# Emptying the product banks of gates and output projection through ScalarE

## The chip, the cores and the metric

The kernel runs on one core of a Trainium2 chip. The metric is the device time of one execution in microseconds (us). The engines are named as in the profile: PE is TensorE (matmuls and transposes), PEld its weight loads, DVE is VectorE, ACT is ScalarE, POOL is GpSimd, SP is SyncE, which issues DMAs here. PE writes only to PSUM, which has eight banks of 128 x 512 float32 in this kernel's use; a bank can be written anew when everything that reads its old content is done.

## The reference

One layer of a decoder trunk with 1024 tokens and 1024 features, all in float32:

```python
h = rms_norm(x, norm_in_gain) * (1.0 + scale) + shift        # scale, shift, gate from silu(c) @ w_ada
q, k, v, z_attn, xbc, dt_raw, z_ssm = split(h @ w_in)
o = stick_breaking_attention(q, k, v)                        # 16 heads of 64
y_attn = rms_norm(o, sb_norm_gain) * silu(z_attn)
xs, b, c = split(silu(causal_depthwise_conv(xbc)))
y = ssd_scan(xs, softplus(dt_raw), a, b, c, d_skip)          # 16 heads, chunks of 128
y_ssm = rms_norm(y * silu(z_ssm), ssm_norm_gain)
x = x + gate * (concat([y_attn, y_ssm]) @ w_out)
return rms_norm(x, norm_f_gain)
```

The attention weight of query t on key s is sigmoid(z_ts) times the product of (1 - sigmoid(z_tj)) over s < j < t.

## The kernel before

Every product with a weight matrix is made of three float32r matmuls (high x high, high x low, low x high parts), 128 x 128 weights against 512 columns, accumulated over eight k tiles. `inproj_f` makes one 128-row block of the input projection: two banks (`b` = 0, 1), eight k-steps of three matmuls each, and after each bank its `evac`. `inproj_v` makes the value columns, `outproj` the output projection.

Up to about 305 us the kernel computes the normalised input, the convolution inputs and the state-space scan. From then on (`pinned[0] = True`) every instruction stands in the order in which the program emits it on its engine. That order comes from a loop over the eight pairs of heads, `ROUND`: `scores(p, i)` makes the logits of query block i in the four `pz` banks, ScalarE turns them into two sigmoids (queue `late["A"]`), VectorE scans the products along the keys and multiplies (`scan`, `weights`, queue `late["V"]`). `turned(p, i)` transposes the weights on PE and ScalarE copies them back, `values(p, i)` multiplies them with v. Between these, `fill` and `side_step` run the side jobs of `SIDES`, one k-step at a time: `z` (attention gate), `g` (SSM gate, in round 0 only), `q` (q and k of the next pair), `v`, in round 6 `t` (`turn`, the last gate with the exchange of h for w_out in SBUF) and in round 7 `o` (`out_ssm`, the SSM half of the output projection). The attention half follows after the loop. `after(delay, fn)` emits something when the planner's clock `tick` has gone on by `delay`; `late` items are emitted at a planned rate per engine.

PSUM banks are in four pools: `pj` has two banks, for all projections; `pz` four, for the scores; `pt` and `pv` one each, for transposes and for the attention's values. A `turned` of more than four 128-column blocks ("wide") needs a second bank besides `pt` and takes it from `pj`. When it may start is a rule on `left`, the planned time that the projection bank in work still needs:

```python
            while wide and side_left() and left[0] >= 0.0 and not 1.3 < left[0] < (2.2 if slow[0] else 3.6):
                side_step()
```

`slow` is set by the jobs whose bank VectorE empties (`by_v=True` of `zgate` and `gate_ssm`, and `outproj`). Such a bank has two readers: ScalarE's sigmoid or tanh, and VectorE's product with it (line 959 and line 848); of `out_ssm` it has one, VectorE's product with a row statistic and the gate (line 1227). Banks of q and k (`qk`) are read by two ScalarE instructions when pinned: the high part and a full copy into the buffer `th`, and VectorE subtracts from the copy.

`turn` holds two `pj` banks (`pss`) at once, since it goes over the k tiles once to free h: as each k is done for both banks, `split_w` writes rows of w_out in its place. The first bank of `out_ssm` is taken from `pz`, and the loop holds `scores(7, 7)` back until that bank's evacuation is emitted (`hooks["first"]`).

Of the kernel before, what the change touches and what calls it, by code (L numbers as in the profile page):

```python
# [8 lines left out]
F32 = mybir.dt.float32  # L9
# [5 lines left out]
P = 128  # L15
# [11 lines left out]
def hybrid_layer_kernel(  # L27
# [66 lines left out]
    def bank(pool, tag):  # L94
        return mk(pool, tag, [P, HALF])

    eps_t = const("eps_t", [P, 2])
# [83 lines left out]

    left, slow = [0.0], [False]

    h_hi, h_lo = [None] * KT, [None] * KT

# [105 lines left out]
            K(T.matmul(ps, w[:, ws], h[:, b * HALF:(b + 1) * HALF],  # L295
                       start=(k == 0 and n == 0), stop=(k == KT - 1 and n == 2)))

    def inproj_f(col, evac, between=None, by_v=False):


        wts = take(2) if pinned[0] else split_f(load_f(col))
        for b in range(2):
            ps = bank(pj, "pj")
            for k in range(KT):
                mm_f(ps, wts, k, b)
                if pinned[0]:
                    ahead()
                    if b and k % 4 == 3:
                        used()
                left[0], slow[0] = 0.7 * (KT - 1 - k), by_v  # L310
                yield 0.7
            evac(b, ps)
            if between:
                yield between(b)

    def inproj_v(vc, with_dt, v_tiles, dt_raw, extra=None):

        n = 272 if with_dt else 256
        wts = {}
        if not with_dt:  # L320
            for q, (whi, wlo) in enumerate(take(4)):
                for k in range(2):
                    wts[2 * q + k] = (whi, wlo, slice(k * n, (k + 1) * n))
        else:
            for k0 in range(0, KT, 2):
                raw = wraw()
                rv = raw[:, :2 * n].rearrange("p (k f) -> p k f", f=n)
                rs = slice(k0 * P, (k0 + 2) * P)
                SP.dma_start(rv[:, :, :256], w_in[0][rs, C_V + vc * 256:C_V + (vc + 1) * 256]
                             .rearrange("(k p) f -> p k f", p=P))  # L330
                SP.dma_start(rv[:, :, 256:272], w_in[0][rs, C_DT:C_DT + 16]
                             .rearrange("(k p) f -> p k f", p=P))
                whi, wlo = split(raw, 2 * n)
                for k in range(2):
                    wts[k0 + k] = (whi, wlo, slice(k * n, (k + 1) * n))
        for i in range(TB):
            ps = bank(pj, "pj")
            ts_ = slice(i * P, (i + 1) * P)
            for k in range(KT):
                whi, wlo, ws = wts[k]  # L340
                K(T.matmul(ps[:, :n], h_hi[k][:, ts_], whi[:, ws], start=(k == 0), stop=False))  # L341
                K(T.matmul(ps[:, :n], h_hi[k][:, ts_], wlo[:, ws], start=False, stop=False))  # L342
                if i == 0 and extra:
                    extra(ps[:, n:n + TB], k)
                K(T.matmul(ps[:, :n], h_lo[k][:, ts_], whi[:, ws], start=False, stop=(k == KT - 1)))  # L345
                if not with_dt:
                    ahead()
                    if i == TB - 1 and k % 2:
                        used()
                if k == 3:  # L350
                    left[0], slow[0] = 1.4, False
                    yield 1.4
            if i == 0 and extra:
                extra(ps[:, n:n + TB], KT)
            for j in range(2):
                A.copy(v_tiles[j][:, i * P:(i + 1) * P], ps[:, j * P:(j + 1) * P])
            if with_dt:
                A.copy(dt_raw[:, i, :], ps[:, 256:272])
            left[0] = 0.0
            yield 1.4  # L360
# [479 lines left out]
    def gate_ssm(j):  # L840
        box = []

        def evac(b, ps):
            if b == 0:
                box.append(mk(sp, "th", [P, S], bufs=1))
            th, sl = box[0], slice(b * HALF, (b + 1) * HALF)
            A.activation(th[:, sl], ps, AF.Tanh, scale=0.5)
            V.scalar_tensor_tensor(th[:, sl], th[:, sl], 1.0, ps, op0=ALU.add, op1=ALU.mult)
            V.tensor_tensor(xs[j][:, sl], xs[j][:, sl], th[:, sl], op=ALU.mult)

        yield from inproj_f(C_ZS + j * P, evac, by_v=True)
        if pinned[0]:
            after(4.0, lambda: gated(j))
        else:
            gated(j)
# [73 lines left out]
    def qk(p, box):  # L929

        parts = []

        def evac(b, ps):
            if b == 0:
                parts.extend((big(F32R), big(F32R)))
            hi, lo = parts[-2:]
            sl = slice(b * HALF, (b + 1) * HALF)
            A.copy(hi[:, sl], ps)
            if pinned[0]:

                full = mk(sp, "th", [P, S], bufs=1)[:, sl]
                A.copy(full, ps)
                V.tensor_tensor(lo[:, sl], full, hi[:, sl].bitcast(F32), op=ALU.subtract)
            else:
                V.tensor_tensor(lo[:, sl], ps, hi[:, sl].bitcast(F32), op=ALU.subtract)

        for base in (C_Q, C_K):
            yield from inproj_f(base + p * P, evac, gate_row if p == 7 and base == C_Q else None)
        box[p] = parts
# [3 lines left out]
    def zgate_evac(p):  # L953
        def evac(b, ps):
            if b == 0:
                zgs[p] = mk(sp, "bc", [P, S], bufs=4)
            zg = zgs[p][:, b * HALF:(b + 1) * HALF]
            A.activation(zg, ps, AF.Sigmoid)
            V.scalar_tensor_tensor(zg, zg, cols[:, 92 + p:93 + p], ps, op0=ALU.mult, op1=ALU.mult)

        return evac

    def zgate(p):
        yield from inproj_f(C_Z + p * P, zgate_evac(p), by_v=True)

# [77 lines left out]
    def turned(p, i):  # L1045
# [2 lines left out]

        while banks:
            wide = sum(b[2] - b[1] for b in banks[:2]) > 4  # L1050
            while wide and side_left() and left[0] >= 0.0 and not 1.3 < left[0] < (2.2 if slow[0] else 3.6):
                side_step()
            n = 1 if wide and left[0] < 0.0 else 2
            go, banks = banks[:n], banks[n:]
# [57 lines left out]
        A.copy(gate, pg)  # L1112
        return 1.1

    def outproj(w_h, w_l, evac, first=None):

        yt = take(2)
        for b in range(2):
            ps = first if first is not None and b == 0 else bank(pj, "pj")
            sl = slice(b * HALF, (b + 1) * HALF)  # L1120
            for k in range(KT):
                yh, yl = yt[k // 4]
                ks = slice(k % 4 * P, (k % 4 + 1) * P)
                for n, (y, w) in enumerate(((yh, w_h), (yh, w_l), (yl, w_h))):
                    K(T.matmul(ps, y[:, ks], w(k, b), start=(k == 0 and n == 0), stop=(k == KT - 1 and n == 2)))  # L1125
                ahead()
                if b and k % 4 == 3:
                    used()
                left[0], slow[0] = 0.7 * (KT - 1 - k), True
                if k == KT - 1:  # L1130
                    evac(sl, ps)
                yield 0.7
# [8 lines left out]
    def turn():  # L1141
# [46 lines left out]
                load_half(0, lambda q: hp.tile([P, 2, HALF], F32, tag=f"hl{q}", name=f"wor{q}"))  # L1188


        for k, b in [(k, b) for k in range(6) for b in range(2)] + [(6, 0), (7, 0), (6, 1), (7, 1)]:
            for n in range(2):
                K(T.matmul(pss[b], wts[k // 4][n][:, k % 4 * P:(k % 4 + 1) * P],
                           h_hi[k][:, b * HALF:(b + 1) * HALF], start=False, stop=(k == KT - 1 and n == 1)))
            ahead()
            if b:
                wo_h[k] = hp.tile([P, S], F32R, tag=f"hh{k}", name=f"woh{k}")
                split_w(k, 0, V)
                if k % 4 == 3:
                    used()  # L1200
            yield 0.47
            if k == KT - 1:
                zgate_evac(7)(b, pss[b])
# [9 lines left out]
    def out_ssm():  # L1213
# [6 lines left out]
        for i in range(TB):  # L1220
            t3 = []

            def evac(sl, ps):
                hooks["first"] = True
                if not t3:
                    t3.append(mk(sp, "v", [P, S], bufs=3))
                V.scalar_tensor_tensor(t3[0][:, sl], ps, rstds["s"][:, i:i + 1], row["sum"][:, sl],
                                       op0=ALU.mult, op1=ALU.mult)

            yield from outproj(lambda k, b: wo_h[k][:, b * HALF:(b + 1) * HALF],  # L1230
                               lambda k, b: wo_l[k // 2, b][:, k % 2], evac, None if i else bank(pz, "pz"))
            if not x_at:
                load_x2(i)
            t2 = x_at.pop(i)
# [133 lines left out]
    for p in range(9):  # L1368
        for what, i, before in ROUND:
# [4 lines left out]
            elif what == "t":  # L1374
                turned(p + before, i)
            elif what == "f":
                fill(2.0)
            else:
                while p not in box:
                    side_step()  # L1380
                while (p, i) == (7, 7) and "first" not in hooks:
                    side_step()
                scores(p, i)
                fill(4.0 if i != 3 else 2.0)
            if (p, what, i) == (6, "f", 0):
# [126 lines left out]
```

## Time and profile before

| | |
|---|---|
| time, median of 3 runs | 1063.65 us (1063.28 to 1064.63) |
| the profiled execution | 1063.0 us, span of its instructions 1061.3 us |
| granted TensorE clock | 0.999 |
| PE busy | 1039.0 us (98%) |
| DVE busy | 768.0 us (72%) |
| ACT busy | 528.6 us (50%) |
| DMA | 96.15 MB, mean 91 GB/s |
| rounds p = 1 to 7 begin at | 411, 493, 563, 633, 703, 773 and 850 us |

The profile is one execution, recorded on the chip. "Busy" of PE counts pipelined matmuls whose ends are modelled, so short waits hide in it; where it matters, the distance between the starts of two matmuls is taken instead. Nearly all instructions of ACT, DVE and SP carry line 62 (L62), a helper, so groups are told apart by the names of what they write and read: `bc<-bc,cols,pj` writes tile `bc` from `bc`, `cols` and bank `pj`. Of PE, L295 are the input projections, L341 to L345 the values' projection, L1003 the scores, L1066 the transposes of `turned`, L1084 the attention's values, L1182 and L1193 `turn`, L1125 the output projection.

### The profile page before, as it was taken

What the parts mean: (1) busy time and instruction counts of PE and PEld (TensorE: products, weight loads), DVE (VectorE), ACT (ScalarE), POOL (GpSimd) and SP (SyncE); (2) the same over time, 40 slices, a digit from 0 to 9 for tenths busy, and PEclk for the clock granted to TensorE, in tenths of its full rate; (3) what the DMA queues carried; (4) which work ended last, traced back from release to release, by engine and by line L of the source; (5) the groups of instructions that cost most, each with busy time, mean ns of one, the idle gap of its engine ahead of it and who ended that gap; (6) DMA issues with size and microseconds to landing.
All of it is one profiled execution on the core that took longest, in us unless ns stands there. A gap on an engine that the chain in (4) does not pass through costs nothing.

```text
span 1061.3 us, 16252 instructions
## 1 busy us (share of the span) xinstructions
PE 1039.0 (98%) x6317; PEld 844.2 (80%) x6317; DVE 768.0 (72%) x1339; ACT 528.6 (50%) x1162; POOL 2.6 (0%) x23
## 2 busy tenths in 40 slices
PE   7999999999999999999999999999999999999997
PEld 5789888777877787798787987878977777688886
DVE  5728779988848775656787758877668789665554
ACT  5755397676423553563554644646546646410111
POOL 0000000000000000000000000000000000000000
PEclk9999999999999999999999999999999999999999
DMA  9611332223202221101321103211111632665432
GB/s 350 229 41 31 92 112 79 74 95 129 71 20 70 80 70 31 60 21 41 91 59 61 31 21 90 76 35 41 39 52 30 199 97 74 204 210 174 155 110 79
DMA packets 91560, 96.15 MB, mean 91 GB/s; under 512 B 5998, under 2 KB 75994, under 8 KB 91484
## 3 DMA queue, kind: packets, MB, share of 16 engines
q1 hardware_dynamic: 88828, 86.45, 25.9%
q10 hardware_dynamic: 2656, 8.67, 2.4%
q8 instruction: 49, 0.80, 0.3%
q14 instruction: 27, 0.22, 0.1%
HBM read 78.26 MB, written 16.84 MB: 90 GB/s over the span
## 4 chain that ended last, share of the span: by engine, by line
PE 86%; DVE 8%; ACT 2%; issue 2%; DMA 1%; ACTq 0%; DVEq 0%; SPq 0%
PE pj L295 35%; PE pj L1125 13%; PE pv L1084 6%; PE pz L1003 5%; PE pz L553 3%; PE pt L1066 3%; PE pj L345 3%; PE pj L341 3%; PE pj L342 3%; DVE om L62 2%; PE pj L1066 2%; DVE bc L62 2%; PE pz L815 1%; PE pv L829 1%; PE pz L820 1%
## 5 line engine op out<-in xcount | busy, mean ns | idle before, releaser
L295 PE MATMUL pj<-hh,whi 128*128 128x512 f32 x544 | 222.2, 408 | 0.0
L295 PE MATMUL pj<-hh,wlo 128*128 128x512 f32 x544 | 214.1, 394 | 0.0
L295 PE MATMUL pj<-hl,whi 128*128 128x512 f32 x544 | 212.5, 391 | 0.0
L295 PEld LDWEIGHTS pj<-hh,whi 128*128 128x128 f32 x544 | 102.3, 188 | 24.5 <-issue 5.6
L295 PEld LDWEIGHTS pj<-hh,wlo 128*128 128x128 f32 x544 | 102.1, 188 | 22.7 <-issue 0.7
L295 PEld LDWEIGHTS pj<-hl,whi 128*128 128x128 f32 x544 | 102.5, 188 | 19.1 <-issue 1.0
L62 DVE TENSOR_TENSOR wlo<-raw,whi 128x512 fp32r<-128x512 f32 (+1 forms) x109 | 75.4, 692 | 23.1 <-ACT whi L62 16.7
L62 ACT COPY be<-pt 128x512 f32<-128x512 f32 (+2 forms) x98 | 47.1, 499 | 82.7 <-PE pt L1066 79.7
L62 ACT ACTIVATE be<-pz 128x255 f32<-128x255 f32 (+5 forms) x160 | 84.6, 531 | 0.0
L62 DVE TENSOR_TENSOR_SCAN om<-om 128x896 f32<-128x896 f32 (+6 forms) x56 | 71.9, 1285 | 2.0
L62 DVE TENSOR_TENSOR_SCAN bc<-bc 128x896 f32<-128x896 f32 (+6 forms) x56 | 71.9, 1285 | 2.0
L62 DVE TENSOR_TENSOR_SCAN om<-om,ident 128x128 f32<-128x128 f32 x64 | 26.9, 421 | 62.3 <-ACT om L62 62.2
L62 ACT ACTIVATE om<-pz 128x512 f32<-128x512 f32 (+1 forms) x96 | 48.0, 500 | 36.1 <-PE pz L1003 36.1
L341 PE MATMUL pj<-whi,hh 128*128 128x256 f32 (+1 forms) x224 | 65.1, 291 | 0.0
L1003 PE MATMUL pz<-big,big 64*128 64x512 f32 (+2 forms) x576 | 63.5, 354 | 1.1 <-ACT be L62 0.9
L345 PE MATMUL pj<-whi,hl 128*128 128x256 f32 (+1 forms) x224 | 64.4, 288 | 0.0
L342 PE MATMUL pj<-wlo,hh 128*128 128x256 f32 (+1 forms) x224 | 63.6, 284 | 0.0
L62 ACT ACTIVATE th<-v 128x1024 f32<-128x1024 f32 (+2 forms) x9 | 8.5, 943 | 103.7 <-DVE v L62 103.7
L1003 PEld LDWEIGHTS pz<-big,big 64*128 64x128 f32 x576 | 46.2, 184 | 17.3 <-issue 10.2
L62 DVE TENSOR_TENSOR be<-be,bc 128x1024 f32<-128x1024 f32 (+6 forms) x62 | 55.4, 894 | 1.3
L295 PE MATMUL pj<-hh,st 128*128 128x512 f32 x160 | 55.4, 399 | 0.0
L62 ACT ACTIVATE bc<-pz 128x512 f32<-128x512 f32 (+1 forms) x96 | 53.7, 559 | 0.0
(303 smaller groups left out, 2166.8 us busy)
## 6 DMA issues: line engine op xcount, KB each, us to landing
raw<-in_w_in_dram SPq DMA_DIRECT2D x98, 256.0 KB, 2.8
be<-acT_d ACTq DMA_DIRECT2D x16, 512.0 KB, 3.8
big<-in_x_dram SPq DMA_DIRECT2D x10, 512.0 KB, 6.9
aw<-in_w_ada_dram SPq DMA_DIRECT2D x16, 256.0 KB, 4.6
u_d<-big SPq DMA_DIRECT2D x8, 512.0 KB, 2.6
y_d<-bc SPq DMA_DIRECT2D x8, 512.0 KB, 3.0
raw<-in_w_ada_dram SPq DMA_DIRECT2D x16, 256.0 KB, 2.7
raw<-u_d SPq DMA_DIRECT2D x16, 256.0 KB, 2.9
```

Of the source, the lines that this page charges most:

```text
L62: return lambda *args, **kw: K(op(*args, **kw))
L295: K(T.matmul(ps, w[:, ws], h[:, b * HALF:(b + 1) * HALF], start=(k == 0 and n == 0), stop=(k == KT - 1 and n == 2)))
L341: K(T.matmul(ps[:, :n], h_hi[k][:, ts_], whi[:, ws], start=(k == 0), stop=False))
L342: K(T.matmul(ps[:, :n], h_hi[k][:, ts_], wlo[:, ws], start=False, stop=False))
L345: K(T.matmul(ps[:, :n], h_lo[k][:, ts_], whi[:, ws], start=False, stop=(k == KT - 1)))
L553: K(T.matmul(acc[f][:, c0:c1], w[:, f * P:(f + 1) * P], h[:, sl], start=(k == 0 and n == 0 and c0 == 0), stop=(k == KT - 1 and n == 2)))
L815: K(T.matmul(po, xd[:, 0, h, :], m[:, h, :], start=True, stop=(ch == 0)))
L820: K(T.matmul(po, st[:, h, :], abc[:, h, :], start=False, stop=True))
L1003: K(T.matmul(zs[b][e][:, z0:z0 + mw], a[r, i * P:(i + 1) * P], k_[r, c0:c0 + mw], start=(n == 0), stop=(n == 2)))
L1066: K(T.transpose(room[:, (used_ + j - j0) * P:(used_ + j - j0 + 1) * P], be[:, j * P:(j + 1) * P], ident))
L1084: K(T.matmul(pav[p][64 * e:64 * e + 64, (q0 + u) * P:(q0 + 2) * P], vs[p][:, j * P + 64 * e:j * P + 64 * e + 64], tl[e][:, u:2, x0 + j * P ...
L1125: K(T.matmul(ps, y[:, ks], w(k, b), start=(k == 0 and n == 0), stop=(k == KT - 1 and n == 2)))
```

## The change

A helper `emptied` copies a bank to a new two-fold SBUF buffer `hf` on ScalarE, with a per-row scale where one is given. The products of `zgate_evac`, of `gate_ssm` (where pinned) and of `out_ssm` read the copy instead of the bank; `qk` uses the helper for the copy that it had. The `slow` flag goes, and with it the narrower rule for a wide `turned`. The first bank of `out_ssm` comes from `pj`, and `scores(7, 7)` no longer waits for its evacuation. In `turn` the last three k tiles go over the first bank and then over the second, and `split_w` of the first half is emitted 1.2 us later on the planner's clock. The scratch space for dynamic DMA is halved.

```diff
+    def emptied(ps, scale=None):
+        full = mk(sp, "hf", [P, HALF], bufs=2)
+        if scale is None:
+            A.copy(full, ps)
+        else:
+            A.activation(full, ps, AF.Copy, scale=scale)
+        return full
...
-                left[0], slow[0] = 0.7 * (KT - 1 - k), by_v
+                left[0] = 0.7 * (KT - 1 - k)
...
             A.activation(th[:, sl], ps, AF.Tanh, scale=0.5)
-            V.scalar_tensor_tensor(th[:, sl], th[:, sl], 1.0, ps, op0=ALU.add, op1=ALU.mult)
+            full = emptied(ps) if pinned[0] else ps
+            V.scalar_tensor_tensor(th[:, sl], th[:, sl], 1.0, full, op0=ALU.add, op1=ALU.mult)
...
             A.copy(hi[:, sl], ps)
             if pinned[0]:
-                full = mk(sp, "th", [P, S], bufs=1)[:, sl]
-                A.copy(full, ps)
-                V.tensor_tensor(lo[:, sl], full, hi[:, sl].bitcast(F32), op=ALU.subtract)
+                V.tensor_tensor(lo[:, sl], emptied(ps), hi[:, sl].bitcast(F32), op=ALU.subtract)
...
             A.activation(zg, ps, AF.Sigmoid)
-            V.scalar_tensor_tensor(zg, zg, cols[:, 92 + p:93 + p], ps, op0=ALU.mult, op1=ALU.mult)
+            V.scalar_tensor_tensor(zg, zg, cols[:, 92 + p:93 + p], emptied(ps), op0=ALU.mult, op1=ALU.mult)
...
-            while wide and side_left() and left[0] >= 0.0 and not 1.3 < left[0] < (2.2 if slow[0] else 3.6):
+            while wide and side_left() and left[0] >= 0.0 and not 1.3 < left[0] < 3.6:
...
-            ps = first if first is not None and b == 0 else bank(pj, "pj")
+            ps = bank(pj, "pj")
...
-        for k, b in [(k, b) for k in range(6) for b in range(2)] + [(6, 0), (7, 0), (6, 1), (7, 1)]:
+        for k, b in ([(k, b) for k in range(5) for b in range(2)] + [(k, 0) for k in range(5, KT)]
+                     + [(k, 1) for k in range(5, KT)]):
...
-                split_w(k, 0, V)
+                after(1.2, lambda k=k: split_w(k, 0, V))
...
-                V.scalar_tensor_tensor(t3[0][:, sl], ps, rstds["s"][:, i:i + 1], row["sum"][:, sl],
-                                       op0=ALU.mult, op1=ALU.mult)
+                full = emptied(ps, rstds["s"][:, i:i + 1])
+                V.tensor_tensor(t3[0][:, sl], full, row["sum"][:, sl], op=ALU.mult)
...
-                while (p, i) == (7, 7) and "first" not in hooks:
-                    side_step()
...
-    nc = _bacc.Bacc("TRN2", target_bir_lowering=False, num_devices=1, dynamic_dma_scratch_size=8192)
+    nc = _bacc.Bacc("TRN2", target_bir_lowering=False, num_devices=1, dynamic_dma_scratch_size=4096)
```

More of the change, by code (lines that the diff above doesn't have):

```diff
@@ L182, in weave @@
                 live.remove(it)
-    left, slow = [0.0], [False]
+    left = [0.0]
     h_hi, h_lo = [None] * KT, [None] * KT
@@ L296, in mm_f, with inproj_f @@
                        start=(k == 0 and n == 0), stop=(k == KT - 1 and n == 2)))
-    def inproj_f(col, evac, between=None, by_v=False):
+    def inproj_f(col, evac, between=None):
         wts = take(2) if pinned[0] else split_f(load_f(col))
@@ L350, in inproj_v @@
                 if k == 3:
-                    left[0], slow[0] = 1.4, False
+                    left[0] = 1.4
                     yield 1.4
@@ L847, in evac @@
             A.activation(th[:, sl], ps, AF.Tanh, scale=0.5)
-            V.scalar_tensor_tensor(th[:, sl], th[:, sl], 1.0, ps, op0=ALU.add, op1=ALU.mult)
+            full = emptied(ps) if pinned[0] else ps
+            V.scalar_tensor_tensor(th[:, sl], th[:, sl], 1.0, full, op0=ALU.add, op1=ALU.mult)
             V.tensor_tensor(xs[j][:, sl], xs[j][:, sl], th[:, sl], op=ALU.mult)
-        yield from inproj_f(C_ZS + j * P, evac, by_v=True)
+        yield from inproj_f(C_ZS + j * P, evac)
         if pinned[0]:
@@ L958, in evac @@
             A.activation(zg, ps, AF.Sigmoid)
-            V.scalar_tensor_tensor(zg, zg, cols[:, 92 + p:93 + p], ps, op0=ALU.mult, op1=ALU.mult)
+            V.scalar_tensor_tensor(zg, zg, cols[:, 92 + p:93 + p], emptied(ps), op0=ALU.mult, op1=ALU.mult)
         return evac
     def zgate(p):
-        yield from inproj_f(C_Z + p * P, zgate_evac(p), by_v=True)
+        yield from inproj_f(C_Z + p * P, zgate_evac(p))
     GROUPS = {7: ((7, 0, 512, 0, 0), (7, 512, 512, 1, 0)), 6: ((6, 0, 512, 0, 0), (6, 512, 384, 1, 0)),
@@ L1113, in gate_row, with outproj @@
         return 1.1
-    def outproj(w_h, w_l, evac, first=None):
+    def outproj(w_h, w_l, evac):
         yt = take(2)
         for b in range(2):
-            ps = first if first is not None and b == 0 else bank(pj, "pj")
+            ps = bank(pj, "pj")
             sl = slice(b * HALF, (b + 1) * HALF)
@@ L1128, in outproj @@
                     used()
-                left[0], slow[0] = 0.7 * (KT - 1 - k), True
+                left[0] = 0.7 * (KT - 1 - k)
                 if k == KT - 1:
@@ L1223, in evac @@
             def evac(sl, ps):
-                hooks["first"] = True
                 if not t3:
                     t3.append(mk(sp, "v", [P, S], bufs=3))
-                V.scalar_tensor_tensor(t3[0][:, sl], ps, rstds["s"][:, i:i + 1], row["sum"][:, sl],
-                                       op0=ALU.mult, op1=ALU.mult)
+                full = emptied(ps, rstds["s"][:, i:i + 1])
+                V.tensor_tensor(t3[0][:, sl], full, row["sum"][:, sl], op=ALU.mult)
             yield from outproj(lambda k, b: wo_h[k][:, b * HALF:(b + 1) * HALF],
-                               lambda k, b: wo_l[k // 2, b][:, k % 2], evac, None if i else bank(pz, "pz"))
+                               lambda k, b: wo_l[k // 2, b][:, k % 2], evac)
             if not x_at:
```

## The prediction

> **What bounds the kernel now.** I read the page first: busy time, then the chain that ended last.
>
> ```profile
> PE 1039.0 (98%) x6317; PEld 844.2 (80%) x6317; DVE 768.0 (72%) x1339; ACT 528.6 (50%) x1162; POOL 2.6 (0%) x23
> ...
> PE 86%; DVE 8%; ACT 2%; issue 2%; DMA 1%; ACTq 0%; DVEq 0%; SPq 0%
> ```
>
> TensorE (PE) is busy for 98% of the span and holds 86% of the chain. The change takes no matmul away, so all it can win is the time in which PE stands still for another engine. VectorE (DVE) is the only other engine with a real share of the chain. The second view is the busy time by stage; its columns are us, then busy time and instruction count of PE, PEld, DVE, ACT and POOL, then clock and DMA.
>
> ```profile
> 493.00:563.00 70.00, 68.62 (x416) 53.71 (x416) 57.34 (x101) 36.92 (x86) 0.00 (x0) 1.00 0.25 72
> 563.00:633.00 70.00, 70.00 (x520) 60.14 (x518) 47.64 (x83) 38.05 (x99) 0.00 (x0) 1.00 0.11 35
> ...
> 850.00:925.00 75.00, 72.33 (x448) 55.59 (x447) 61.22 (x103) 34.64 (x83) 0.00 (x0) 1.00 0.36 117
> ```
>
> These are rounds p=2, p=3 and p=7 of the attention loop. Round 3 has no gate among its side jobs and PE has no gap in it (70.00 of 70.00). Round 2 has two gate projections (z2, z3) and PE loses 1.4 us; round 7, with the SSM output projection beside it, loses 2.7 us. The third view says for whom PE waits from 305 us, where the hand-ordered part begins, to 935 us (us in total, times, longest):
>
> ```profile
> PE pj L1066 <- DVE bc L62: 3.0, 4, 1.0
> PE pj L1066 <- DVE v L62: 1.4, 1, 1.4
> PE pj L1066 <- DVE th L62: 1.3, 2, 0.9
> PE pj L1066 <- DVE be L62: 1.1, 1, 1.1
> PE pz L1003 <- ACT be L62: 0.9, 1, 0.9
> PE pt L1066 <- ACT be L62: 0.5, 1, 0.5
> PE pj L1125 <- ACT be L62: 0.3, 1, 0.3
> ```
>
> The first four rows are one thing: a transpose of `turned` that needs a `pj` bank, eight times, 6.8 us. One of them in the timeline of each engine (start, us, instruction, in brackets the idle time before it):
>
> ```profile
> 502.83 0.60 PE L1066 MATMUL pt<-ident,bs 128*128 128x128 f32 x4
> 503.83 0.66 PE L1066 MATMUL pj<-ident,bs 128*128 128x128 f32 x4 [0.41 <-DVE bc L62]
> ```
>
> ```profile
> 499.62 0.60 ACT L62 ACTIVATE bc<-pj 128x512 f32<-128x512 f32 x1 [1.65 <-PE pj L295]
> ```
>
> ```profile
> 500.60 0.42 DVE L62 TENSOR_TENSOR_SCAN bc<-bc,ident 128x128 f32<-128x128 f32 x1
> 501.06 2.08 DVE L62 TENSOR_TENSOR_SCAN bc<-bc 128x896 f32<-128x896 f32 x1
> 503.06 0.72 DVE L62 SCALAR_TENSOR_TENSOR bc<-bc,cols,pj 128x512 f32<-128x512 f32 x1
> ```
>
> The gate's bank was complete at 499.6. ScalarE (ACT) had its sigmoid at 500.2, but the second reader, VectorE's product, stood behind two scans in VectorE's order and ended at 503.78; PE resumed 0.05 us later. So VectorE's queue holds the bank, not the work on it. In the same kernel q and k banks are emptied by two ScalarE instructions and only then touched by VectorE:
>
> ```profile
> 798.09 0.58 ACT L62 CAST big<-pj 128x512 fp32r<-128x512 f32 x1 [2.12 <-PE pj L295]
> 798.57 0.59 ACT L62 COPY th<-pj 128x512 f32<-128x512 f32 x1
> ```
>
> ```profile
> 800.83 0.60 PE L1066 MATMUL pt<-ident,be 128*128 128x128 f32 x4
> 801.27 0.60 PE L1066 MATMUL pj<-ident,be 128*128 128x128 f32 x4
> ```
>
> There the bank is free 1.1 us after its last matmul, and the `pj` transposes start 0.44 us after the `pt` ones with no gap. Against that 0.44, the 1.00 us from 502.83 to 503.83 is a loss of 0.56, not the 0.41 that the bracket tells: the modelled end of a matmul hides about 0.15 us of each wait.
>
> **The change part by part.**
>
> *Gate and SSM output banks emptied by ScalarE (16 z banks, 8 ssm-gate banks, 16 output banks).* Eight waits go: 6.8 + 8 x 0.15 = 8.0 us. What is late next at these places is the ScalarE copy. At 503.83 it would end about 500.7 (sigmoid from 499.62, copy 0.48 behind it as in the q/k pair, 0.59 long), 2.6 us before PE wants the bank at 503.27. VectorE's own lateness stays, and the transposes need its weights: the tightest stretch is round 7, where VectorE is busy 61.2 of 75 us, yet there the last weights before the long gap are done like this:
>
> ```profile
> 907.64 0.69 DVE L62 TENSOR_TENSOR bs<-bs,bc 128x511 f32<-128x511 f32 x1
> ```
>
> ```profile
> 917.27 0.66 PE L1066 MATMUL pt<-ident,bs 128*128 128x128 f32 x4
> ```
>
> 9 us of cover, more than all that PE gains in that round, so the gain is not handed back to a wait for weights.
>
> Price of the copies, from the groups by form:
>
> ```profile
> L62 ACT COPY th<-pj 128x512 f32<-128x512 f32 x28 | 18.2, 652 | 0.0
> L62 ACT ACTIVATE big<-big,cols 128x512 f32<-128x512 f32 x8 | 5.3, 722 | 0.0
> ```
>
> ```profile
> L62 DVE SCALAR_TENSOR_TENSOR bc<-bc,cols,pj 128x512 f32<-128x512 f32 x16 | 11.8, 735 | 2.7 <-ACT bc L62 2.7
> L62 DVE SCALAR_TENSOR_TENSOR sq<-raw,cact,sq 128x512 f32<-128x512 f32 x14 | 10.3, 739 | 0.0
> ```
>
> 24 plain copies at 0.65 and 16 with a scale column at about 0.72 are 27 us more on ScalarE, spread over 630 us in which it is about half idle. VectorE gains nothing: a product with a bank (735 ns) and one with SBUF alone (739 ns) take the same. The 28 q/k copies exist already and only change their buffer: nothing. VectorE's product now waits for the copy, 0.48 us behind the sigmoid; behind it in VectorE's order stand scans and weight splits. The 2.7 us in three waits show that VectorE seldom stands there even today, and the 9 us cover it. A matmul takes 0.227 us where nothing disturbs PE, by this piece of the chain in order of time (start, us):
>
> ```profile
> 934.89 108.29 PE pj L1125 x477
> ```
>
> The `hf` buffer has two copies, so a copy waits for the product two banks (48 matmuls, 10.9 us) back, while the product above lagged 4.2 us behind its bank.
>
> Bounds for PE's loss to a busier ScalarE: nothing (q/k banks, round 3 without a gap) up to 40 x 0.48 = 19 us, if every copy ends up in front of a transpose copy that PE waits for. I take 0.5 us, next to the q/k rows, which are the same two instructions from the same banks.
>
> *The `slow` flag goes.* After a gate or output step a wide `turned` may now start with `left` up to 3.5, three k-steps behind an evacuation, where it had to wait for 2.1. That is the q/k rule: at 800.83 it stands exactly three k-steps behind the bank that was emptied from 798.09, with no gap. The steps that it used to pull forward come later; the matmuls stay the same. Nothing, covered by the 1.1 us emptying against 2.0 + 0.44 us of PE work.
>
> *`turn`: wider split of the two banks, weight copies 1.2 us later.*
>
> ```profile
> 832.66 0.62 ACT L62 CAST woh<-wor 128x512 fp32r<-128x512 f32 x1 [0.51 <-DMA wor<-in_w_out_dram]
> 833.18 0.26 ACT L62 COPY be<-pt 128x128 f32<-128x128 f32 x1
> ...
> 838.09 0.60 ACT L62 ACTIVATE bc<-pj 128x512 f32<-128x512 f32 x1 [0.28 <-PE pj L1193]
> ```
>
> ```profile
> 833.50 0.44 PE L1066 MATMUL pt<-ident,be 128*128 128x128 f32 x2 [0.50 <-ACT be L62]
> ...
> 838.79 0.39 PE L1125 MATMUL pz<-woh,st 128*128 128x512 f32 x1
> ```
>
> The transposed block's copy stands behind a weight copy that waits; with the weight copy later this 0.5 + 0.15 us goes. I take 0.6.
>
> *First output bank in `pj` and no wait for it before `scores(7, 7)`.* Today it takes one of the four `pz` banks, and `scores(7, 7)`, which needs four, stops in the middle:
>
> ```profile
> 850.34 1.19 PE L1003 MATMUL pz<-big,big 64*128 64x512 f32 x7
> 852.47 0.97 PE L1003 MATMUL pz<-big,big 64*128 64x512 f32 x5 [0.94 <-ACT be L62]
> ```
>
> Gone: 0.94 + 0.15 = 1.1 us. In exchange the first output matmul (838.79) needs the bank of `pss[0]`. The new order puts 6 matmuls of `pss[1]`, 1.36 us, between; sigmoid and copy need 1.1 us plus perhaps one weight copy (0.48) in front: 0 to 1.2 us lost, I take 0.3. The delayed weight copies of k = 5 to 7 land after both sigmoids and copies, and their low parts follow on VectorE behind scans; the output needs k = 5 only 5 x 0.68 = 3.4 us after its start. 0 to 1.5 us, I take 0.4. The last row of the waits (0.3, an output bank waiting for a transpose copy) should go as the other `pj` bank is free sooner: 0.3.
>
> *Scratch size, first scores two k-steps earlier, no DMA moved past another:* nothing. No transfer of the page is issued by GpSimd.
>
> Sum: 8.0 + 0.6 + 1.1 + 0.3 - 0.5 - 0.3 - 0.4 = 8.8 us. The profiled execution took 1063.0 us (span 1061.3), so 1054.2; the median shown, 1063.65, stands 0.65 above it: **1054.9 us**.
>
> **The rivals.**
>
> *ScalarE becomes the late one (slower).* The place is the single `pt` bank: its copy stands in ScalarE's order behind an evacuation, now two instructions of it. Price 0.48 us a bank, at most 19.2 us against the other terms' gain of 9.3, which is 1073.5; it decides from 9.3 / 40 = 0.23 us a bank on. For it: after a score block eight sigmoids fill ScalarE. Against it: 28 q/k banks do this now and round 3 shows no gap. With three quarters of the price it gives 1068.7. Chance 0.06.
>
> *The wait only changes its name.* VectorE holds 8% of the chain; if transposes moved up by the looser rule meet weights that are not ready, PE stands for VectorE as before: 0 to 2 us gained, 1062.5. Against it are the 9 us of cover. The Trainium skill (VectorE: DVE Perf Modes, Rules for kernel authors) speaks for this side: take a matmul result straight from PSUM, or copy it first only where many operations follow. By that rule 40 copies that serve one product each buy nothing, and with only the two other waits gone the time would be about 1062. The trace says otherwise for the bank, not for the engine's time: 735 against 739 ns agree with the rule, the 8.0 us of waits are what it leaves out. Chance 0.10.
>
> *Half of it.* The places where the interleave shifts make new short waits, above all `turn` to output (bounds 1.2 + 1.5) and round 7: 3 to 5 us of the 10 come back, 1058 to 1060.5. Chance 0.20.
>
> **How the numbers follow.** The forecast case has 0.64 with its own range 1052.5 (all 10.0 gone, nothing new, 1 us of hidden waits besides) to 1057.5. For 8 in 10 the range takes in the half case: 1051.5 to 1061. A change under 0.2% (2.1 us) can't be told from none. Forecast and half case are faster (0.84), the renamed wait is nearly all "same" (0.09 of its 0.10), ScalarE late and the remaining 0.01 are slower (0.07).
>
> **What would show it.** Right: the four rows of `pj L1066 <- DVE` gone from PE's waits; `hf<-pj` copies on ScalarE ending about 1.1 us after the bank; rounds 2, 4 and 6 with PE as full as round 3; twelve score matmuls in one piece at the start of round 7. Wrong: rows `L1066 <- ACT` or `L1125 <- ACT` in place of those, a gap at the first output matmul or at its k = 5, or transposes that wait for `be` and `bs` products.

## The result and the profile after

The changed kernel took 1052.12 us (median of 4 runs, 1051.72 to 1052.59) against 1063.47 us for the kernel before (4 runs): a ratio of 0.9892 with a 95% interval of 0.9875 to 0.9909. The forecast was 1054.9 us with a range of 1051.5 to 1061, so 8.8 us of gain were forecast and 11.3 us came. The time lies inside the range, 0.6 us above its lower end, and just below the narrower 1052.5 to 1057.5 that was given for the forecast case itself.

The page of the kernel after, its busy times and the shares of its chain:

```profile
PE 1036.0 (99%) x6317; PEld 844.3 (80%) x6317; DVE 766.6 (73%) x1339; ACT 549.4 (52%) x1202; POOL 2.7 (0%) x23
...
PE 94%; DMA 4%; ACT 1%; DVE 1%; SPq 0%; issue 0%
```

The matmuls are the same 6317. ScalarE has 40 instructions and 20.8 us more, VectorE 1.4 us less; its share of the chain fell from 8% to 1%, TensorE's rose from 86% to 94%. The waits of PE from 305 us to 925 us, the view in which the kernel before had four rows of `pj L1066 <- DVE` (L1066 is L1074 in the new file, L1003 is L1011, L1125 is L1133, L1084 is L1092):

```profile
PE pj L1133 <- ACT be L62: 0.3, 1, 0.3
PE pz L1011 <- DVE big L62: 0.2, 1, 0.2
```

All four rows are gone, and so are the wait in `turn` and the one in the scores. Round 2, in which PE lost 1.4 us, has no gap any more (491 to 561 us, the columns as in the prediction), and the twelve score matmuls at the start of round 7 stand in one piece:

```profile
491.00:561.00 70.00, 70.00 (x430) 55.02 (x428) 58.06 (x103) 39.66 (x92) 0.00 (x0) 1.00 0.26 72
```

```profile
840.74 1.67 PE L1011 MATMUL pz<-big,big 64*128 64x512 f32 x12
```

The place that the prediction showed in the timeline looks like this now, first ScalarE, then VectorE, then PE:

```profile
497.69 0.60 ACT L62 ACTIVATE bc<-pj 128x512 f32<-128x512 f32 x1 [1.65 <-PE pj L304]
498.18 0.58 ACT L62 COPY hf<-pj 128x512 f32<-128x512 f32 x1
```

```profile
499.12 2.08 DVE L62 TENSOR_TENSOR_SCAN bc<-bc 128x896 f32<-128x896 f32 x1
501.12 0.73 DVE L62 SCALAR_TENSOR_TENSOR bc<-bc,cols,hf 128x512 f32<-128x512 f32 x1
```

```profile
499.54 0.60 PE L1074 MATMUL pt<-ident,bs 128*128 128x128 f32 x4
499.97 0.60 PE L1074 MATMUL pj<-ident,bs 128*128 128x128 f32 x4
```

VectorE's product is as late as before: it begins 3.4 us after the sigmoid (501.12 against 497.69), as it did at 503.06 against 499.62. But it reads `hf`, and the bank was free at 498.76, so the `pj` transposes begin 0.43 us after the `pt` ones.

Where the 11.3 us came from is read best from work that both kernels do in the same order. The large block of `values` of each round (56 matmuls) is one piece of the chain in order of time (start, us). Before:

```profile
405.81 5.77 PE pv L1084 x56
487.25 5.77 PE pv L1084 x56
557.61 5.77 PE pv L1084 x56
626.97 5.77 PE pv L1084 x56
697.60 5.77 PE pv L1084 x56
766.96 5.77 PE pv L1084 x56
843.03 5.77 PE pv L1084 x56
911.58 5.77 PE pv L1084 x56
```

After:

```profile
403.86 5.77 PE pv L1092 x56
485.32 5.77 PE pv L1092 x56
553.88 5.77 PE pv L1092 x56
623.25 5.77 PE pv L1092 x56
691.82 5.77 PE pv L1092 x56
761.19 5.77 PE pv L1092 x56
835.04 5.77 PE pv L1092 x56
900.30 5.77 PE pv L1092 x56
```

| up to this block | lead of the kernel after, us | won since the block before |
|---|---|---|
| round 0 (four SSM gates, one z gate) | 1.95 | 1.95 (0.2 of it before 311 us) |
| round 1 (q, k, v, one z gate) | 1.93 | 0.0 |
| round 2 (two z gates) | 3.73 | 1.8 |
| round 3 (q, k, v) | 3.72 | 0.0 |
| round 4 (two z gates) | 5.78 | 2.1 |
| round 5 (q, k, v) | 5.77 | 0.0 |
| round 6 (z gate, `turn`) | 7.99 | 2.2 |
| round 7 (output projection) | 11.28 | 3.3 |

From 911 us (900 us after) to the end nothing changes: the spans differ by 11.3 us too (1061.3 and 1050.0). But for the 0.2 us before 311 us, the gain lies exactly in the rounds in which PE waited.

### The profile page after: what moved, and what is told of

It is laid out like the page before. It is cut to its first block, busy times and chain, and to the rows that moved or that the text cites. A ratio compares the mean times of both kernels' runs of the same rounds, so it can differ in the third digit from the quotient of the medians.

```text
span 1050.0 us, 16348 instructions
## 1 busy us (share of the span) xinstructions
PE 1036.0 (99%) x6317; PEld 844.3 (80%) x6317; DVE 766.6 (73%) x1339; ACT 549.4 (52%) x1202; POOL 2.7 (0%) x23
## 4 chain that ended last, share of the span: by engine, by line
PE 94%; DMA 4%; ACT 1%; DVE 1%; SPq 0%; issue 0%
PE pj L304 41%; PE pj L1133 16%; PE pv L1092 6%; PE pz L1011 6%; PE pt L1074 4%; PE pj L354 3%; PE pj L350 3%; PE pj L351 3%; PE pj L1074 2%; PE pz L562 2%; PE pz L824 2%; PE pv L838 1%; PE pz L829 1%; PE pj L1467 1%; DMA aw<-in_w_ada_dram 1%; PE pz L811 1%
## 5 line engine op out<-in xcount | busy, mean ns | idle before, releaser
L1011 PE MATMUL pz<-big,big 64*128 64x512 f32 (+2 forms) x576 | 63.0, 354 | 0.2 <-DVE big L62 0.2
L1011 PEld LDWEIGHTS pz<-big,big 64*128 64x128 f32 x576 | 46.1, 184 | 15.8 <-issue 10.0
L1092 PE MATMUL pv<-be,v 128*64 128x256 f32 (+1 forms) x512 | 53.3, 361 | 0.0
```

The costliest lines, as they stand in the source:

```text
L1011: K(T.matmul(zs[b][e][:, z0:z0 + mw], a[r, i * P:(i + 1) * P], k_[r, c0:c0 + mw], start=(n == 0), stop=(n == 2)))
L1092: K(T.matmul(pav[p][64 * e:64 * e + 64, (q0 + u) * P:(q0 + 2) * P], vs[p][:, j * P + 64 * e:j * P + 64 * e + 64], tl[e][:, u:2, x0 + j * P ...
```

## The experiments

All ratios are against the kernel before, run on the same chip beside the kernel tried, with 95% intervals. Where a kernel is compared with the kernel after, the runs are of different batches, in which the kernel before took 1063.06 to 1063.79 us. Differences under 1 us are read from starts in the profiles.

**The copies alone** (kernel before with `emptied` for gates, q/k and output, and the halved scratch space; everything else as before):

```diff
+    def emptied(ps, scale=None): ...
-            V.scalar_tensor_tensor(zg, zg, cols[:, 92 + p:93 + p], ps, op0=ALU.mult, op1=ALU.mult)
+            V.scalar_tensor_tensor(zg, zg, cols[:, 92 + p:93 + p], emptied(ps), op0=ALU.mult, op1=ALU.mult)
...  (gate_ssm and out_ssm likewise; narrow rule, old turn, first bank in pz and its wait kept)
```

> The kernel before with the ScalarE copies alone: the narrow rule for wide transposes, the order in turn, the first output bank in pz and the wait before scores(7, 7) stay. Theory (VectorE's queue holds the bank; the copy lets it go): the eight pj waits go, 8.0 to 8.5 us, the waits in turn (0.5) and in scores(7, 7) (0.9) stay in the profile: 1055 (1054 to 1056). Rival (the looser rule did it): 1061 or more.

Measured: 1053.2 us, ratio 0.9908 (0.9894 to 0.9921). It is better than the 1054 to 1056 that were expected: its span of 1051.3 us is 10.0 us shorter than that of the kernel before, of the 11.3 of the whole change. Its waits of PE in the same stretch:

```profile
PE pt L1074 <- ACT be L62: 0.7, 2, 0.4
PE pj L1133 <- ACT be L62: 0.3, 1, 0.3
PE pz L1011 <- DVE big L62: 0.2, 1, 0.2
```

The wait in `turn` stayed, as expected, and is now two waits of 0.7 us in all. The one in `scores(7, 7)` did not: although the first output bank is still in `pz`, the wait went with the copies. In the kernel before VectorE reads that bank only from 852.68 to 853.42 us; here ScalarE has emptied it at 844.06, and the eighth score matmul starts at 844.11. Through round 5 its `values` blocks stand within 0.1 us of those of the kernel after, with the narrow rule; so up to there the looser rule is worth nothing once the copies are there. Of the other 1.3 us, 1.0 are lost in round 6, where `turn` has its old order, and 0.3 in round 7, where it was not tried which of the remaining edits wins them.

**The looser rule alone** (kernel before, VectorE still empties the banks):

```diff
-            ... not 1.3 < left[0] < (2.2 if slow[0] else 3.6):
+            ... not 1.3 < left[0] < 3.6:
```

> The kernel before with the looser rule alone (a wide turned may start at left up to 3.5 beside every job), VectorE still empties the banks. Theory: the transposes ask for the same late banks up to 1.4 us sooner, so the pj waits for VectorE grow: from 6.8 us to 10 or more, time 1066 (1063.5 to 1072). Rival (the rule did it): 1061 or less.

Measured: 1074.4 us, ratio 1.0103 (1.0089 to 1.0116), 11 us slower, more than the middle of what was expected and over its upper end of 1072. The waits of PE and one of them in the timeline:

```profile
PE pj L1066 <- DVE bc L62: 7.2, 4, 2.0
PE pj L1066 <- DVE th L62: 4.0, 2, 2.2
PE pj L1066 <- DVE be L62: 3.6, 2, 2.4
```

```profile
507.36 0.60 PE L1066 MATMUL pt<-ident,bs 128*128 128x128 f32 x4
509.73 0.66 PE L1066 MATMUL pj<-ident,bs 128*128 128x128 f32 x4 [1.77 <-DVE bc L62]
```

```profile
508.95 0.72 DVE L62 SCALAR_TENSOR_TENSOR bc<-bc,cols,pj 128x512 f32<-128x512 f32 x1
```

The three rows of waits alone hold 14.8 us, where the kernel before had 6.8 in all such rows. The transposes ask sooner for banks that VectorE frees as late as ever: its product ends 4.16 us after the start of the sigmoid (505.51 to 509.67), exactly as in the kernel before (499.62 to 503.78). The 0.56 us lost here before (502.83 to 503.83, less 0.44) are now 1.93 (507.36 to 509.73, less 0.44), 1.37 us more, which is two k-steps of 0.68.

**`turn` and the first bank alone** (kernel before with the new order of k, the delayed `split_w`, the first output bank in `pj`, no wait before `scores(7, 7)`):

> The kernel before with the new order and the later weight copies in turn, and the first output bank in pj without the wait before scores(7, 7); no copies, narrow rule. Theory: the waits of 0.5 (turn) and 0.9 (scores(7, 7)) go, some 2.0 us of PE time with what the row hides, but the first output bank now waits until VectorE has emptied pss[0], which took 3.5 us after its last matmul against 1.36 us of other work: about 2 us back, 1063 (1061 to 1065), with a new PE wait for DVE at the first L1125 matmul. Rival (these parts pay by themselves): 1061.0 or less without that wait.

Measured: 1064.7 us, ratio 1.0008 (0.9999 to 1.0017): no difference. The waits show both sides of it:

```profile
PE pj L1125 <- DVE bc L62: 2.2, 1, 2.2
```

The waits in `turn` and in the scores were gone, and this new one stood at the first output matmul, behind VectorE's product on `pss[0]`, which ended at 840.41, 0.06 us before PE went on. By the `values` blocks round 6 lost 1.6 us and round 7 won 1.7. As expected, these edits pay only where ScalarE empties the bank: there the two in `turn` are worth 1.3 us (below).

**The copies on VectorE** (kernel after, `V.tensor_copy` and `V.tensor_scalar_mul` in `emptied` for gates and output):

> The kernel after, but the 40 copies of gate and output banks are made by VectorE (tensor_copy, tensor_scalar_mul) in place of ScalarE; q and k as in the kernel after. Theory (what counts is that the bank's last reader does not stand in VectorE's queue): the pj waits for DVE come back, and with the looser rule and 40 x 0.4 to 0.7 us more on VectorE they are at least those of before: 1064 or more (to 1075). Rival (any copy to SBUF helps, as the product no longer reads PSUM): within 3 us of the kernel after.

Measured: 1081.17 us, ratio 1.0164 (1.0143 to 1.0186), beyond the expected upper end. PE's waits:

```profile
PE pj L1076 <- DVE hf L62: 19.2, 11, 3.0
PE pj L1135 <- DVE hf L62: 2.1, 1, 2.1
```

So it is not the copy to SBUF that helps but the queue in which the bank's last reader stands. The size of the loss is not that of the waits alone. The profiled execution has a span of 1082.0 us, 32 more than the kernel after; the twelve waits hold 21.3 us in the rows, about 23 with the 0.15 us that each one hides. Most of the rest goes with a lower granted clock, an estimate from these rows: it was 0.95 in the 103 us from 311 to 414 us and 0.96 in the 82 us from 781 to 863 us, which makes some 8 us. In the other rounds it was 1.00, as in the kernel after from 311 to 932 us. In the stretch with the longest wait it was 0.76 (columns as in the prediction's second view):

```profile
360.00:370.00 10.00, 7.02 (x29) 5.61 (x28) 9.25 (x18) 3.42 (x6) 0.00 (x0) 0.76 0.20 71
```

Whether the waits lower the clock was not tried.

**Every copy made twice on ScalarE** (kernel after):

```diff
             A.copy(full, ps)
+            A.copy(full, ps)
```

> The kernel after with every copy of a bank to hf made twice on ScalarE (40 for gates and output, 28 for q and k: 68 more, 0.48 us each in a row, 33 us more on ScalarE). Theory (ScalarE has room and a bank is wanted 2.5 us after its last matmul at the soonest, against 1.6 us for three instructions): 1052 to 1054, no pj wait over 0.5 us. Rival (ScalarE is close to being the late one): 0.23 us a bank or more, 16 us over the kernel after, 1060 or more, with PE waits for ACT at L1074 and L304.

Measured: 1054.67 us, ratio 0.9912 (0.9898 to 0.9926), 2.5 us more than the kernel after, 0.7 us above the expected range, and far from the 1060 of the rival. The waits:

```profile
PE pj L1076 <- ACT hf L62: 0.9, 2, 0.4
PE pj L1135 <- ACT hf L62: 0.4, 1, 0.4
```

Of 33 us more on ScalarE 2.6 us reach PE from the first scores on (spans 1052.7 and 1050.0, 0.1 of it earlier). They arise almost wholly at these three waits, by the `values` blocks 0.6 us in each of rounds 3 and 5 and 0.9 in round 6. ScalarE has room for the copies, but not without end.

**The old `turn` in the kernel after** (old order of k, `split_w` at once):

> The kernel after with the old order of k tiles in turn and split_w at once. Theory (these two edits pay 0.9 us in turn and cover the emptying of pss[0]): the PE waits for the pt copy in turn come back (0.7 us) and the first L1133 matmul waits some 0.2 to 0.5 us for ScalarE: 1052.9 to 1053.6. Rival (they do nothing): within 0.3 us of the kernel after, by the spans of the profile.

Measured: 1053.95 us, ratio 0.9906 (0.9891 to 0.992), a little over the expected range. 0.5 us of its longer span arise before the hand-ordered part; 1.3 us arise between the score blocks at 767 and 841 us, and two waits name most of them:

```profile
PE pt L1074 <- ACT be L62: 0.4, 1, 0.4
...
PE pj L1133 <- ACT hf L62: 0.3, 1, 0.3
```

The first is the transposes' bank behind a weight copy, the second `pss[0]` at the first output matmul.

**Copies for the attention gate alone** (kernel before, 16 banks, and the halved scratch space):

> The kernel before with the ScalarE copy for the 16 attention-gate banks alone. Theory (each wait belongs to the one bank that VectorE holds): rounds 2, 4 and 6 lose their waits (1.8 + 2.0 + 1.3 = 5.1 us), rounds 0 and 7 keep theirs: 1058.4. Rival (VectorE's queue gets shorter everywhere, so that rounds 0 and 7 gain too): 1055 or less.

Measured: 1057.63 us, ratio 0.994 (0.9927 to 0.9952), span 1055.8: 5.5 us won where 5.1 were expected. Rounds 2, 4 and 6 won 1.8, 2.1 and 1.6; rounds 0 and 7 kept their waits:

```profile
PE pj L1075 <- DVE v L62: 1.5, 1, 1.5
PE pj L1075 <- DVE th L62: 1.3, 2, 0.9
PE pz L1012 <- ACT be L62: 0.9, 1, 0.9
PE pt L1075 <- ACT be L62: 0.5, 1, 0.5
```

Each wait belongs to one bank of VectorE's; a shorter VectorE queue elsewhere is not the cause. The scratch space does nothing either: rounds 0, 1, 3, 5 and 7 take as long as in the kernel before, to 0.1 us.

**Can the last wait go?** Three tries on the kernel after. The first narrows the rule from below:

```diff
-            ... not 1.3 < left[0] < 3.6:
+            ... not 2.0 < left[0] < 3.6:
```

> The kernel after with a wide turned only at left 2.1 to 3.5 (lower bound 2.0 in place of 1.3), so that the transposes' own use of a pj bank ends sooner before the next projection bank. Theory (the last pj wait, 0.3 us in the view and 0.66 us by starts, is an output bank that meets a transpose copy started two k-steps before): it goes, 1051.5. Rival (the interleave shifts elsewhere): 1052 or more with other short waits.

Measured: 1055.56 us, ratio 0.9921 (0.9907 to 0.9935), 3.4 us worse than the kernel after. The wait of 0.3 us stayed, and others came:

```profile
PE pj L1074 <- ACT hf L62: 0.7, 2, 0.4
PE pt L1074 <- ACT be L62: 0.7, 3, 0.3
```

These rows hold 1.4 us of the 3.4; where the rest is lost stays open.

The second copies the `pj` part of a small wide transpose before the `pt` part:

```diff
-            for to, from_ in copies:
+            small = wide and len(go) == 2 and go[1][2] - go[1][1] <= 2
+            for to, from_ in (copies[::-1] if small else copies):
```

> The kernel after, with the copies of a wide turned in the other order where its pj part is one or two blocks (256 columns or less): the pj bank is copied out first, the pt bank 0.3 to 0.4 us later. Theory (the last pj waits, 0.2 and 0.46 us by starts, are output banks behind the longer pt copy): these go, 0.6 us, and pt is wanted late enough; span 1049.4, time 1051.6. Rival (pt, a single bank, is the scarcer one): new PE waits for ACT at L1074 of the pt bank, span 1050 or more.

Measured: 1054.27 us, ratio 0.991 (0.9896 to 0.9924); the rival holds. The wait for `pj` is gone and the single `pt` bank is waited for instead, in the timeline at

```profile
542.66 0.66 PE L1074 MATMUL pt<-ident,be 128*128 128x128 f32 x4 [0.26 <-ACT be L62]
```

Its span is 2.8 us over that of the kernel after, 1.05 us of which arise before 311 us, where the two kernels do the same. From there on it loses 1.0, 1.0 and 0.5 us in rounds 2, 4 and 6 and wins 0.8 in round 7. With the four banks of the first q and k copied too:

> The same, and the four banks of the first q and k, before the hand-ordered part, are also emptied by a ScalarE copy. Theory: the wait of the first scores for VectorE's low part (0.2 us in the view, 0.4 by starts) does not go, since the scores need that low part itself; the copy makes it 0.3 us later: span 0 to 0.4 us over e9_swap. Rival (VectorE's read of the bank is what is late): span 0.3 us under it.

Measured: 1054.17 us, ratio 0.991 (0.9896 to 0.9924). The span is 0.3 us under that of e9_swap, but from the first scores at 310 us to the end it lost 0.4 us against it; the wait of those scores for VectorE's low part grew from 0.2 to 0.6 us:

```profile
PE pz L1011 <- DVE big L62: 0.6, 1, 0.6
```

It does not go by a copy, as the scores need the low part itself.

The third makes the swap in round 7 alone (`small = p == 7 and wide and ...`):

> The kernel after, with the pj part copied out first only in round 7, where the output projection runs beside. Theory (in round 7 the pj bank is the scarce one, in the gate and q/k rounds pt is): the 0.77 us that e9_swap won between 860 and 910 us stay and nothing is lost before: from the same start of the hand-ordered part the end comes 0.7 us sooner than in the kernel after, span 1049.3, time 1051.4. Rival (pt waits come in round 7 too): no gain.

Measured: 1051.14 us, ratio 0.9884 (0.9868 to 0.9901), span 1049.4. From 860 to 910 us it wins 0.75 us over the kernel after and loses nothing elsewhere. PE's waits in the hand-ordered part:

```profile
PE pz L1011 <- DVE big L62: 0.2, 1, 0.2
```

This is the fastest of the kernels tried. Its lead of 1 us over the kernel after is small against their runs (1050.95 to 1052.61 and 1051.72 to 1052.59); what carries it is the profile.

## Why the prediction was right, and what was mis-sized

*The eight waits for a `pj` bank.* Right in cause and place; 8.0 us forecast, 8.7 measured (rounds 0, 2 and 4: 1.75 from the first scores on, 1.8, 2.1; 1.4 at the last z gate of round 6; 1.6 at the bank of 906 us). The part that a row hides was taken from one wait as 0.15 us; over the eight it is (8.7 - 6.8) / 8, about 0.24. The copies alone remove the waits, the copies on VectorE bring them back.

*`turn`.* 0.6 forecast, 0.8 measured (the rest of round 6's 2.2, by the scores before `turn`, at 802.50 and now at 795.31). The short piece of 0.25 us ahead of the row that was quoted had been left out of the term. Beside the copies the edits are worth more, 1.0 to 1.3 us, by e1_copies and e6_after_old_turn.

*The scores of round 7.* 1.1 forecast, 1.65 measured from 843 to 860 us. The wait was put down to the bank in `pz`. Both edits remove it: e3_turn_first by the other bank, e1_copies by the copy with the bank left in `pz`. So the term could have been won without the other bank, and the prediction did not see that. What the rest of the 1.65 comes from was not tried by itself; in the new order the first output bank is no longer cut off a second time between `values` and the scores, which may be it.

*ScalarE's own lateness.* 0.5 taken from bounds of 0 and 19; measured 0, as no PE wait for a copy is left in the view and rounds 1, 3 and 5 take as long as before. Taking the q/k rows as the nearest was the right choice; the doubled copies show that a second helping would have cost 2.6. The price of the copies, 27 us, adds up the lengths of instructions, which overlap in the trace (one begins at 498.18 us, the one before it ends at 498.29); ScalarE's busy time grew by 20.8 us.

*The new places.* The first output bank (0.3) and the weights of k = 5 (0.4) cost nothing: `turn` and output run on in the chain of the kernel after without a gap between them.

```profile
825.84 5.02 PE pj L1202 x22
830.87 4.17 PE pj L1133 x18
```

One term was wrong: the output bank that waits for a transpose copy (0.3) did not get free sooner and stayed; only the swapped copies (e9_swap, e10_swap_qk0, e11_swap_r7) removed it. The two terms and ScalarE's 0.5 were insurance of 1.2 us that was not needed, the three terms above were too small by 1.4, the output bank takes off 0.3, and 0.2 arise before 311 us: these are the 2.5 us by which the gain was forecast too low.

*The looser rule.* Taken as nothing, and nothing beside the copies through round 5, where it can be read alone. The prediction did not say what the rule costs without them: 11 us.

*The rivals.* "ScalarE becomes the late one" and "half of it" fell with the waits that they needed. "The wait only changes its name" fell too: VectorE's product is still 3.4 us late, and no transpose waited for weights. The cover for that had been read at one place in round 7, called the tightest stretch; by its own view VectorE is as full in round 2 (57.3 of 70 us, 82%, as 61.2 of 75), so the place proved less than it was taken for. The time of the half case, 1058 to 1060.5, is also up to 0.6 us above what its words give (1054.9 and 3 to 5 us more). The Trainium skill (VectorE: DVE Perf Modes, Rules for kernel authors) would take a matmul result straight from PSUM unless many operations follow. For VectorE's own time the trace agrees: the product takes 742 ns from the copy and 735 from the bank. For the kernel's time e1_copies decides against it: 40 copies for one product each won 10 us, by freeing the bank.

```profile
L62 DVE SCALAR_TENSOR_TENSOR bc<-bc,cols,hf 128x512 f32<-128x512 f32 x16 | 11.9, 742 | 3.5 <-ACT hf L62 3.5
```

## What to carry to other kernels

When the busiest engine waits for a buffer, look at which queue the buffer's last reader stands in, and not only at how long that reader takes: an extra copy on an engine that gets to it at once can be worth more than it costs. A rule of the schedule that fits one way of emptying a buffer (here the narrow rule for VectorE's banks) should be tried together with the other way; alone, the looser rule lost 11 us, and the new `turn` gained nothing. Of two buffers that the same engine empties one after the other, empty that one first which is wanted first; which one that is changed here from round to round, and it was worth 0.75 us in one round.

## What had not been expected

An engine at half load is not free for any amount of work. The doubled copies put ScalarE at 379.87 us busy in the 625 us from 300 to 925, against 346.37 in the kernel after, and 2.6 us of that reached PE (us, then busy time and count of ACT, clock, DMA):

```profile
300.00:925.00 625.00, 379.87 (x867) 1.00 0.23 70
```

And kernels whose instructions are the same, in the same order, up to there differ in when the first scores begin: 310.39 us in the kernel after, 1.05 us later in e9_swap. Some 0.6 us of it are there by 26 us, where the first loads land, and 0.4 come at 228 us, where PE waits 0.9 us for VectorE instead of 0.4. Why these differ stays open; it is the reason for comparing such small differences from one piece of work to another inside the traces, and not by spans.
